# A decoder trunk in split float32: buffers of the MLP contraction laid where the next activations go, and pipelined quads

## The chip, the cores and the metric

The kernel runs on one core of a Trainium2 chip. The metric is the device time of one execution in microseconds (us); lower is better.

## What is computed

Two layers of a hybrid decoder act on a sequence of 1024 tokens with 1024 features, in float32. Both layers end in the same way; only that part is touched by the change.

```python
h = h + rmsnorm(m, ln_mix_post[layer])            # m: mixer output (attention, or a recurrence)
u = rmsnorm(h, ln_mlp_pre[layer])
f = jnp.square(jax.nn.relu(u @ mlp_w_up[layer])) @ mlp_w_down[layer]
h = h + rmsnorm(f, ln_mlp_post[layer])
e = rmsnorm(p[layer] @ ple_w_proj[layer], ple_norm[layer])
h = h + e * jax.nn.sigmoid(h @ ple_w_gate[layer])
```

`mlp_w_up` is 1024 x 4096, `mlp_w_down` 4096 x 1024, `ple_w_gate` 1024 x 1024.

## The kernel before, in words

**Split float32.** Every operand of a matmul is held as a high and a low part: ScalarE (ACT) casts it (line 117), VectorE (DVE) subtracts the cast from it (line 118). A product is then three matmuls, high-high, high-low and low-high (`mm3`, lines 149 to 151), each 128 x 128 by 128 x 512.

**Strassen-like MLP.** Both MLP products use a 2 x 2 block scheme with seven products in place of eight: A11, A12, S1, S2, S3, S4 and A22 name the sums of weight blocks, and the activations have seven matching factors (B11, B21, B22, T1 to T4). The factors of the input of the up product live in `comb`: four of them in the slots of the turned activations (`quart`, in the pool that `open_u` makes on the right side of the memory), three in the pool `ux`.

**Stages of one layer's end.** (1) `mix_out`: for each of eight token blocks `out_row` finishes the mixer's output product onto a partial sum loaded from memory, adds the residual and norms; `combine` turns the result by eight 128 x 128 transposes and writes factors into `comb`. Between them stand six products of the up stage, A11 and A12 of the first three of eight groups of 512 hidden features ("quads"): these three are *led*. A list, `plan`, sets the order in which these are written. (2) `mlp_up`: per quad seven products of 24 matmuls (five for a led quad). The two running banks are `b` and `c`; each value of `b` is read before the next product adds to it. DVE and ACT form hidden values, square them, form T1 to T4 and store all seven factors to memory (`keep`). For quads 0 and 1 `keep` splits each factor first into a pair of tiles `t` (three buffers) and stores both halves with DMAs that GpSimd (POOL) issues; for the others it stores the float32 tile with a DMA that SyncE (SP) issues. (3) `mlp_down`: four chunks of two quads, in the order 1, 2, 3, 0, seven products of 48 matmuls per chunk. `step` loads each factor, through a tile `c` and a split, or for chunk 0's quads as the stored pair; hidden tiles and half of the weights live in a pool `dn`, which is opened when `ux` and the activations' slots are closed. (4) gate: `add_norm` for all eight token blocks, their turning into fresh activation slots (`to_u`, 64 transposes, line 185), and 16 products of 24 matmuls, with a sigmoid behind each.

**What sets the order.** The kernel is written in one sequence, and a scheduler decides, per engine, the order in which instructions stand; each engine then runs its own in that order. A tile's buffer is given out again when its last reader is done. Four tiles `c0` to `c3` pass from hand to hand through a free list (`Free`); a led quad holds one for its partial sum `m1` and one for `u2`, and gives both back at its end. The scratch tiles of `mix_out` and the weight tiles of `mlp_up` (`wq`, `S`) share memory.

Of the kernel before, what the change touches and what calls it, by code (L numbers as in the profile page):

```python
# [17 lines left out]
P = 128  # L18
# [21 lines left out]
def tile_hybrid_trunk(  # L40
# [45 lines left out]
    def open_u(name, TA):  # L86
        up = tc.alloc_tile_pool(name=name, bufs=1, side="right", reuse_waits="tile")
        upools.append(up)
        for th, kh in ((1 - TA, 1), (1 - TA, 0), (TA, 1), (TA, 0)):
            quart[th, kh] = tuple(up.tile([P, 4, 512], F32R, name=f"u{x}{th}{kh}") for x in "hl")  # L90
# [88 lines left out]
    def to_u(tb, n):  # L179
        th, j = divmod(tb, 4)  # L180
        for hf in range(2):
            tp = any_bank()
# [719 lines left out]
    class Layer:  # L902
        def __init__(self, layer, TA, last):
# [5 lines left out]
            self.hidS = {(i, q): [dram.tile([P, D], F32R, name=f"hid{x}{layer}_{i}_{q}") for x in "hl"]  # L909
                         for i in range(7) for q in range(2)}  # L910
# [11 lines left out]
        def mix_out(self, wap, kpairs, src, part, order):  # L922
# [11 lines left out]
            with tc.tile_pool(name=f"pre{layer}", bufs=1, reuse_waits="tile") as mp:  # L934
                wslots.append((mp, "wBh", "wBl", 1, 1))
                wcount[0] = 0
                gains = [mp.tile([P, D], F32, name="gain", bufs=2) for _ in range(2)]
                bcast_row(gains[0], ln_mix_post[layer:layer + 1, :])
                w = [[stage_k(wap, r, 2, nh * 512, 512) for r in kpairs] for nh in range(2)]
# [6 lines left out]
                def out_row(tb):  # L946
                    a = mp.tile([P, D], F32, name="a", bufs=3)
                    nc.sync.dma_start(out=a, in_=part[tb])
# [9 lines left out]
                    vec(a, acc, a, ALU.add)  # L958
# [7 lines left out]
                def combine(tb):  # L966
# [23 lines left out]
                    vec(t1, p1, s1, ALU.subtract)  # L990
                    nc.scalar.copy(out=t3, in_=p1)
# [3 lines left out]
                    split(H[B22], L[B22], p2)  # L995
                    split(H[T3], L[T3], t3)
                    vec(t4, s2, t2, ALU.subtract)
                    split(H[T1], L[T1], t1)
                    split(H[T4], L[T4], t4)

                leads = []
                for q in range(NLEAD):
                    leads += self.lead_steps(q, mp)
                plan = [(out_row, 0), (out_row, 1), (combine, 0), (out_row, 2), (combine, 1), (out_row, 3),
                        (combine, 2), (out_row, 4), (combine, 3), (out_row, 5), None, (combine, 4),
                        (out_row, 6), None, (combine, 5), (out_row, 7), None, (combine, 6), None, None, None,
                        (combine, 7)]
                for step in plan:
                    if step is None:
                        leads.pop(0)()  # L1010
                    else:
                        step[0](order[step[1]])
                del wslots[3:]
# [26 lines left out]
        def loader(self, view, place):  # L1040
            got = {}

            def A(m, k):
                if (m, k) not in got:
                    pool, name, nb = place(m, k)
                    t = pool.tile([P, WE if name == "wraw" else D], F32, name=name, bufs=nb)[:, 0:D]
# [47 lines left out]

# [133 lines left out]
        def mlp_down(self, macc):  # L1228
# [5 lines left out]
            for c in range(chunks):  # L1234
                if c:
                    self.begin(c)
# [178 lines left out]
```

## Time and profile before

| quantity | value |
|---|---|
| median of 3 runs | 2764.43 us (2760.29 to 2765.16) |
| the profiled execution's own time | 2754.74 us |
| its span, first to last instruction | 2752.9 us |
| TensorE (PE) busy | 2531.9 us, 92% of the span |
| DVE, ACT, POOL busy | 60%, 46%, 10% |
| mean granted TensorE clock | 0.964 |

A wait row names who waited, for which engine's result, and then the total in us, how often, and the longest. In a timeline row the bracket at the end is the idle time of the engine just before that instruction, and what ended it. A window row gives the busy time of each engine in that stretch. The granted clock of 1.00 is 2.4 GHz, 0.50 is 1.2 GHz.

### The profile page before, as it was taken

How to read it: one execution, taken by the hardware profiler on the slowest of the kernel's cores; microseconds unless marked ns; L12 is line 12 of the kernel's file. 1: busy time of each engine (PE TensorE's matmuls, PEld its weight loads, DVE VectorE, ACT ScalarE, POOL GpSimd, SP SyncE). 2: the span in 40 equal slices, each digit the busy share in tenths (PEclk: the TensorE clock that was granted, in tenths of full speed). 3: DMA queues.
4: the chain of work that ended last, by engine and by line, in shares of the span. 5: the costliest groups of instructions: out<-in, count | busy, mean ns of one | idle time of the engine just before them, and what ended most of it. 6: DMA issues, size and time to landing. Idle time of an engine off the chain costs nothing. (4 is left out here: it accounts for less than half of the span.)

```text
span 2752.9 us, 31458 instructions
## 1 busy us (share of the span) xinstructions
PE 2531.9 (92%) x11681; PEld 2051.0 (75%) x11681; DVE 1656.4 (60%) x2075; ACT 1266.9 (46%) x1867; POOL 274.4 (10%) x422
## 2 busy tenths in 40 slices
PE   8899999987869998999989999997879998999989
PEld 7687888765657776777868788876657776777867
DVE  5565666665757555667564455645757555677562
ACT  4454556654535444333333366554535444433331
POOL 1312233211011000000200000001011000000210
PEclk9999999988889999999999999998889999999999
DMA  4756543335556437442753321245656437442752
GB/s 155 211 152 186 174 128 120 115 115 214 206 176 222 153 124 281 160 145 85 251 193 116 135 78 58 92 146 200 205 176 222 153 130 282 154 145 81 254 193 99
DMA packets 236733, 446.24 MB, mean 162 GB/s; under 512 B 17939, under 2 KB 125564, under 8 KB 236580
## 3 DMA queue, kind: packets, MB, share of 16 engines
q1 hardware_dynamic: 220452, 385.51, 42.2%
q0 software_dynamic: 16128, 58.73, 6.4%
q8 instruction: 92, 1.51, 0.2%
q14 instruction: 61, 0.50, 0.1%
HBM read 301.94 MB, written 142.23 MB: 161 GB/s over the span
## 5 line engine op out<-in xcount | busy, mean ns | idle before, releaser
L150 PE MATMUL sc<-wAl,hh 128*128 128x512 f32 x864 | 346.6, 401 | 7.5 <-DVE wAl L118 7.4
L149 PE MATMUL sc<-wAh,hh 128*128 128x512 f32 x864 | 333.4, 398 | 17.0 <-ACT wAh L117 15.9
L151 PE MATMUL sc<-wAh,hl 128*128 128x512 f32 x864 | 344.0, 398 | 0.0
L149 PE MATMUL sc<-xh,wAh 128*128 128x512 f32 x384 | 158.3, 412 | 65.9 <-DVE c L878 35.9
L149 PEld LDWEIGHTS sc<-wAh,hh 128*128 128x128 f32 x864 | 163.3, 189 | 59.9 <-ACT wAh L117 17.5
L150 PEld LDWEIGHTS sc<-wAl,hh 128*128 128x128 f32 x864 | 163.4, 189 | 58.9 <-DVE wAl L118 20.8
L149 PE MATMUL sc<-uh,wAh 128*128 128x512 f32 x464 | 185.6, 400 | 9.0 <-ACT wAh L117 9.0
L151 PEld LDWEIGHTS sc<-wAh,hl 128*128 128x128 f32 x864 | 163.5, 189 | 37.1
L150 PE MATMUL sc<-ul,wAh 128*128 128x512 f32 x464 | 183.8, 396 | 0.0
L151 PE MATMUL sc<-uh,wAl 128*128 128x512 f32 x464 | 183.1, 395 | 0.0
L117 ACT CAST hh<-c 128x1024 fp32r<-128x1024 f32 x80 | 83.6, 1048 | 203.7 <-PE sc L150 190.4
L118 DVE TENSOR_TENSOR wAl<-wraw,wAh 128x1024 fp32r<-128x1024 f32 (+1 forms) x94 | 120.4, 1282 | 94.4 <-ACT wAh L117 94.0
L151 PE MATMUL sc<-xh,wAl 128*128 128x512 f32 x384 | 154.4, 404 | 2.8 <-DVE wAl L118 2.8
L118 DVE TENSOR_TENSOR wAl<-wq,wAh 128x1024 fp32r<-128x1024 f32 x80 | 97.6, 1220 | 96.7 <-ACT wAh L117 96.6
L117 ACT CAST wAh<-wraw 128x1024 fp32r<-128x1024 f32 (+1 forms) x94 | 98.5, 1048 | 124.2 <-PE sc L150 45.6
L150 PE MATMUL sc<-xl,wAh 128*128 128x512 f32 x384 | 155.2, 404 | 0.0
L118 DVE TENSOR_TENSOR hl<-c,hh 128x1024 fp32r<-128x1024 f32 x80 | 97.5, 1220 | 95.3 <-ACT hh L117 95.3
L117 ACT CAST wAh<-wq 128x1024 fp32r<-128x1024 f32 x80 | 83.8, 1047 | 137.9 <-PE sc L150 132.1
L149 PEld LDWEIGHTS sc<-xh,wAh 128*128 128x128 f32 x384 | 74.5, 194 | 92.1 <-issue 36.7
L149 PE MATMUL mm<-uh,wAh 128*128 128x512 f32 x312 | 126.8, 406 | 9.7 <-ACT st L344 7.4
L404 DVE CUSTOM_DVE_ANT_0 sn<-sc,bias 128x128 f32<-128x128 f32 (+7 forms) x128 | 94.4, 753 | 55.2 <-PE tp L421 23.6
L150 PE MATMUL mm<-ul,wAh 128*128 128x512 f32 x312 | 124.5, 399 | 0.0
(415 smaller groups left out, 6311.8 us busy)
## 6 DMA issues: line engine op xcount, KB each, us to landing
c<-hid SPq DMA_DIRECT2D x84, 512.0 KB
wq<-in_mlp_w_up_dram SPq DMA_DIRECT2D x44, 512.0 KB
hid<-row SPq DMA_DIRECT2D x38, 512.0 KB
wraw<-in_mlp_w_up_dram SPq DMA_DIRECT2D x32, 512.0 KB
hD<-row SPq DMA_DIRECT2D x32, 512.0 KB
hidh<-t POOLq DMA_DIRECT2D x28, 512.0 KB, 3.2
hidl<-t POOLq DMA_DIRECT2D x28, 512.0 KB, 3.5
hh<-hidh POOLq DMA_DIRECT2D x28, 512.0 KB, 5.0
```

Source lines behind the costliest of these rows:

```text
L117: nc.scalar.copy(out=dst_h, in_=src)
L118: nc.vector.tensor_tensor(out=dst_l, in0=src, in1=f32(dst_h), op=ALU.subtract)
L149: nc.tensor.matmul(dst, lh, rh, start=start, stop=False, skip_group_check=onto)
L150: nc.tensor.matmul(dst, lh, rl, start=False, stop=False, skip_group_check=onto)
L151: nc.tensor.matmul(dst, ll, rh, start=False, stop=stop, skip_group_check=onto)
L404: nc.vector.tensor_tensor_reduce(out=sn[:, :w], in0=sps[:, :w], in1=bias, scale=-1.0, scalar=BIG, op0=ALU.add, op1=ALU.min, accum_out=nm)
```

## The change

It does six things in each layer's end. (a) `out_row` loads the partial sum into a tile `c2` or `c3`, not into the tile `a` that later holds the result; a third `out_row` stands ahead of the first `combine`, and `combine` splits in another order. (b) `early_s1` prepares the S1 weights of quad 0 in `mix_out`, from tiles that are free there, and quad 0 runs S1 before S2. (c) Quads are pipelined: A11 of the next quad stands between S3 and A22 of this one. (d) No factor is stored as a pair: all go out as float32 through SP, and the last chunk of the contraction splits its factors like the others; chunks go 0, 1, 2, 3, and T4 gets a tile of its own. (e) The contraction's hidden tiles and one weight pair use the slots of the next activations, its banks have a pool of their own (`k0` to `k3`), and its first product is issued before the old pools are closed. (f) In the last chunk half of the token blocks are normed after A22 and turned between the last products; the gate norms and turns only the other half, two products after the start.

```diff
-                    a = mp.tile([P, D], F32, name="a", bufs=3)
-                    nc.sync.dma_start(out=a, in_=part[tb])
+                    pt = self.cpool.tile([P, D], F32, name=f"c{2 + tb % 2}", bufs=1)
+                    nc.sync.dma_start(out=pt, in_=part[tb])
...
-                plan = [(out_row, 0), (out_row, 1), (combine, 0), (out_row, 2), (combine, 1), (out_row, 3),
+                plan = [(out_row, 0), (out_row, 1), (out_row, 2), (combine, 0), (out_row, 3), (combine, 1),
...
+                        self.early_s1, (combine, 7)]
...
+        def early_s1(self):
+            A = self.loader(self.up_view(0), lambda m, k: (wpool, "wraw", 2))
+            s1 = A(1, 0)
+            vec(s1, s1, A(1, 1), ALU.add)
+            self.w_s1 = self.weights({"S1": lambda: s1}, "S1", A, None)
...
                     def keep(i, t):
-                        if q >= 2:
-                            nc.sync.dma_start(out=self.hidD[i][q], in_=t)
-                            return
-                        h, l = (hp.tile([P, D], F32R, name="t", bufs=3) for _ in range(2))
-                        split(h, l, t)
-                        for d, s in zip(self.hidS[i, q], (h, l)):
-                            nc.gpsimd.dma_start(out=d, in_=s)
+                        nc.sync.dma_start(out=self.hidD[i][q], in_=t)
...
+                    c = pair_bank()
+                    if q == 0:
+                        product(c, "S1", True)
                     product(b, "S2", led)
+                    running(u2)
+                    if q:
+                        product(c, "S1", True)
+                    product(b, "S3", False)
+                    running(u3)
+                    if q + 1 < quads:
+                        start(q + 1)
...
-                    product(c, "S4", False)
+                    product(c, "S4", False, self.first_step if q == quads - 1 else None)
...
-                    vec(c21, c21, t2, ALU.subtract)
-                    keep(T4, c21)
+                    t4 = hp.tile([P, D], F32, name="t", bufs=3)
+                    vec(t4, c21, t2, ALU.subtract)
+                    keep(T4, t4)
...
-            self.chunk = ((2 * c + 2) % (FF // 512), (2 * c + 3) % (FF // 512))
+            self.chunk = (2 * c, 2 * c + 1)
...
+                    slot = (f"uh{TB}1", f"ul{TB}1", f"uh{TB}0", f"ul{TB}0")[self.turn % 4]
+                    both = upools[-1].tile([P, 2, D], F32R, name=slot, bufs=1)
...
                 for jj, b in product("A22", 0, False):
                     onto((0, 1), jj, b, True)
+                    if final:
+                        norms([4 * TA + 2 * jj + r for r in range(2)], rows)
...
+                if final:
+                    turns(1)
+                for jj, b in product("S4", 1, False):
...
+                    if final:
+                        turns(2 - jj)
...
+            bank0 = {}
+            for jj in range(2):
+                b = bank0[0, jj] = self.down_bank(jj).rearrange("p (r d) -> p r d", d=512)
+                self.down_product(self.ops0, b, jj, True)
             self.xpool.release()
             close_u()
...
+                if nh == 0:
+                    norms(order[4:], rows)
...
+                    if nh == 0:
+                        need_u([order[n + 3]] if 1 <= n < 5 else [])
```

TensorE at the end of layer 0's `mix_out`, before (`tp<-ident,a` is the last `combine`; factors `xh`, `xl` are T2, `uh_131`, `ul_132` are T1):

```order
L151 MATMUL sc<-uh_133,wAl 128x512
L975 MATMUL tp<-ident,a 128x128 x8
L149 MATMUL sc<-xh_7569,wAh 128x512
L150 MATMUL sc<-xl_7570,wAh 128x512
L149 MATMUL sc<-uh_131,wAh 128x512
L150 MATMUL sc<-ul_132,wAh 128x512
L151 MATMUL sc<-xh_7569,wAl 128x512
```

and with the change:

```order
L156 MATMUL sc<-uh_133,wAl 128x512
L979 MATMUL tp<-ident,a 128x128 x8
L154 MATMUL sc<-uh_131,wAh 128x512
L155 MATMUL sc<-ul_132,wAh 128x512
L156 MATMUL sc<-uh_131,wAl 128x512
```

The first product after the last turning was S2, which reads T2 and whose weights are a sum of three loads; now a whole S1, which reads T1, stands there first.

DVE at the end of quad 0 and up to the read of quad 1's first bank, before (`c_8428` is quad 0's hidden block B12 in the making, `c_7998` its B21, `t` the pairs that are stored; `c_8646<-sc,c_8217` is quad 1's `u2`):

```order
L118 TENSOR_TENSOR t<-row,t 128x1024
L118 TENSOR_TENSOR wAl<-wraw,wAh 128x1024
L878 TENSOR_TENSOR t<-c_8428,row 128x1024
L878 TENSOR_TENSOR c_8428<-row,c_8428 128x1024
L878 TENSOR_TENSOR row<-row,t 128x1024
L118 TENSOR_TENSOR t<-t 128x1024
L878 TENSOR_TENSOR c_7998<-c_7998,row 128x1024
L118 TENSOR_TENSOR wAl<-wq,wAh 128x1024
L118 TENSOR_TENSOR t<-c_8428,t 128x1024
L118 TENSOR_TENSOR t<-row,t 128x1024
L118 TENSOR_TENSOR t<-c_7998,t 128x1024
L878 TENSOR_TENSOR c_8646<-sc,c_8217 128x1024
```

and with the change (`c_8442`, `c_7976` and `c_8598<-sc,c_8197` are the same three; the first row reads S4's bank):

```order
L883 TENSOR_TENSOR c_8442<-sc,c_8442 128x1024
L123 TENSOR_TENSOR wAl<-wq,wAh 128x1024
L123 TENSOR_TENSOR wAl<-wraw,wAh 128x1024
L883 TENSOR_TENSOR t<-c_8442,row 128x1024
L883 TENSOR_TENSOR wq<-wq,S 128x1024
L883 TENSOR_TENSOR c_8442<-row,c_8442 128x1024
L883 TENSOR_TENSOR t<-row,t 128x1024
L123 TENSOR_TENSOR wAl<-wq,wAh 128x1024
L883 TENSOR_TENSOR t<-c_7976,t 128x1024
L883 TENSOR_TENSOR c_8598<-sc,c_8197 128x1024
```

Every `t<-...,t` of the old piece is the low half of a split; the new piece has none, and its `t` are T1, T2 and T4 themselves.

## Rows read from the trace of the kernel before

**Rows 1.** Busy time by window: start:end, length, PE, PEld, DVE, ACT, POOL, clock, DMA.
```profile
636.00:736.60 100.60, 90.48 (x401) 73.13 (x401) 69.53 (x77) 53.84 (x98) 12.45 (x17) 0.92 0.59 216
736.60:748.10 11.50, 0.01 (x1) 0.00 (x0) 9.00 (x12) 5.34 (x10) 0.00 (x0) 0.70 0.68 228
748.10:813.20 65.10, 42.54 (x168) 32.65 (x169) 42.19 (x37) 22.20 (x22) 7.68 (x14) 0.81 0.59 194
851.50:1067.00 215.50, 210.07 (x889) 166.28 (x890) 113.17 (x96) 100.20 (x98) 2.65 (x5) 1.00 0.47 167
1067.00:1084.50 17.50, 10.68 (x46) 8.29 (x45) 9.53 (x8) 8.04 (x8) 0.00 (x0) 0.94 0.68 248
1286.00:1399.00 113.00, 111.26 (x473) 88.64 (x474) 72.83 (x64) 38.29 (x49) 20.14 (x34) 1.00 0.64 214
1399.00:1418.20 19.20, 10.63 (x58) 9.35 (x56) 17.35 (x21) 10.79 (x21) 1.42 (x3) 0.70 0.68 229
...
2636.70:2655.30 18.60, 10.71 (x58) 8.63 (x56) 17.37 (x21) 11.31 (x21) 1.45 (x3) 0.74 0.72 253
```

**Rows 2.** Waits of PE over the whole span: total us, times, longest.
```profile
PE sc L149 <- DVE c L878: 35.9, 2, 20.2
PE tp L975 <- DVE a L176: 23.5, 3, 8.5
PE tp L185 <- DVE ul L118: 15.8, 7, 4.6
```

**Rows 3.** Timeline of PE, layer 0: start us, duration us, engine, line, instruction.
```profile
735.57 1.03 PE L975 MATMUL tp<-ident,a 128*128 128x128 f32 x8
748.14 0.80 PE L149 MATMUL sc<-xh,wAh 128*128 128x512 f32 x1 [11.54 <-ACT wAh L117]
...
763.41 0.40 PE L149 MATMUL sc<-xh,wAh 128*128 128x512 f32 x1
...
813.21 0.77 PE L149 MATMUL sc<-xh,wAh 128*128 128x512 f32 x1 [20.15 <-DVE c L878]
...
874.01 0.40 PE L149 MATMUL sc<-xh,wAh 128*128 128x512 f32 x1
...
879.61 0.40 PE L151 MATMUL sc<-uh,wAl 128*128 128x512 f32 x1
...
891.41 0.49 PE L149 MATMUL sc<-uh,wAh 128*128 128x512 f32 x1 [0.90 <-ACT wAh L117]
...
1084.55 1.22 PE L149 MATMUL sc<-wAh,hh 128*128 128x512 f32 x2 [6.87 <-ACT wAh L117]
```

**Rows 4.** Timeline of DVE, layer 0, quads 0 and 1.
```profile
760.07 1.22 DVE L878 TENSOR_TENSOR wq<-wq,S 128x1024 f32<-128x1024 f32 x1 [3.73 <-DMA wq<-in_mlp_w_up_dram]
761.22 1.22 DVE L878 TENSOR_TENSOR c<-sc,c 128x1024 f32<-128x1024 f32 x1
...
785.91 1.22 DVE L878 TENSOR_TENSOR c<-sc,c 128x1024 f32<-128x1024 f32 x1
...
810.58 1.23 DVE L118 TENSOR_TENSOR t<-c,t 128x1024 fp32r<-128x1024 f32 x1 [4.79 <-DMA hidh<-t]
811.84 1.22 DVE L878 TENSOR_TENSOR c<-sc,c 128x1024 f32<-128x1024 f32 x1
```

**Rows 5.** Waits of ACT from 780 to 815 us.
```profile
ACT t L117 <- DMA hidl<-t: 12.7, 3, 5.9
```

**Rows 6.** DMA issues: size each, median us from issue to landing.
```profile
hidh<-t POOLq DMA_DIRECT2D x28, 512.0 KB, 3.2
```

**Rows 7.** Timeline of DVE in layer 0's mix_out.
```profile
681.15 1.23 DVE L878 TENSOR_TENSOR a<-sc,a 128x1024 f32<-128x1024 f32 x1 [3.23 <-DMA a<-part]
```

**Rows 8.** The page's costliest groups: count, busy us, mean ns, idle before.
```profile
L117 ACT CAST hh<-c 128x1024 fp32r<-128x1024 f32 x80 | 83.6, 1048 | 203.7 <-PE sc L150 190.4
L118 DVE TENSOR_TENSOR hl<-c,hh 128x1024 fp32r<-128x1024 f32 x80 | 97.5, 1220 | 95.3 <-ACT hh L117 95.3
```

**Rows 9.** Waits of the DMA queue SP from 736 to 850 us.
```profile
SPq L1048 <- DVE wAl L118: 83.3, 9, 34.5
```

More of the change, by code (lines that the diff above doesn't have):

```diff
@@ L1104, in new @@
                     return self.mw.tile([P, D], F32, name="S", bufs=4)
[L1106 to L1129 removed]
+                started = {}
@@ new lines, in start @@
+                def start(q):
+                    A, sums = self.loader(self.up_view(q), place), {}
+                    if q in self.lead:
+                        started[q] = (A, sums, None) + self.lead.pop(q)
+                        return
+                    b = pair_bank()
+                    self.up_product(b, self.weights(sums, "A11", A, new), "A11", True, True)
+                    m1n, m1 = self.c.take()
+                    nc.scalar.copy(out=m1, in_=b)
+                    started[q] = (A, sums, b, m1n, m1)
@@ new lines, in quad, with product, running @@
+                def quad(q):
+                    A, sums, b, m1n, m1 = started.pop(q)
+                    led = b is None
+                    def product(bank_, name, start, before=None):
+                        w = self.w_s1 if q == 0 and name == "S1" else self.weights(sums, name, A, new)
+                        if before:
+                            before()
+                        self.up_product(bank_, w, name, start, True)
+                    def keep(i, t):
+                        nc.sync.dma_start(out=self.hidD[i][q], in_=t)
+                    def running(dst):
+                        if led:
+                            vec(dst, b, m1, ALU.add)
+                        else:
+                            nc.scalar.copy(out=dst, in_=b)
+                    if not led:
@@ L1307, in mlp_and_ple @@
             pairs[0] = 2
-            open_u(f"ug{layer}", 1 if last else 0)
-            order = [4 * TA + j for j in range(4)] + [4 * (1 - TA) + j for j in range(4)]
-            with tc.tile_pool(name=f"gt{layer}", bufs=1, reuse_waits="tile") as mp:
-                wslots.extend([(self.mw, "wq", "S", 4, 4)] * 4)
-                wcount[0] = 3
-                (_, g1), (_, g2), (_, j1), (_, j2) = [self.c.take() for _ in range(4)]
-                bcast_row(g1, ln_mlp_post[layer:layer + 1, :])
-                if not last:
-                    bcast_row(g2, ln_mix_pre[layer + 1:layer + 2, :])
-                halves = [j[:, i * 512:(i + 1) * 512] for j in (j1, j2) for i in range(2)]
+            fill_u(TB)
@@ new lines, in mlp_and_ple @@
+            order = [4 * TA + j for j in range(4)] + [4 * TB + j for j in range(4)]
+            wslots.extend([(self.mw, "wq", "S", 4, 4)] * 4)
+            wcount[0] = 3
+            (_, j1), (_, j2) = self.c.take(), self.c.take()
+            if not last:
+                g2 = self.c.take()[1]
+                bcast_row(g2, ln_mix_pre[layer + 1:layer + 2, :])
+            halves = [j[:, i * 512:(i + 1) * 512] for j in (j1, j2) for i in range(2)]
+            for nh in range(2):
+                cs = slice(nh * 512, (nh + 1) * 512)
+                w = [stage_k(ple_w_gate[layer], kb, 2, nh * 512, 512) for kb in range(0, KB, 2)]
+                if nh == 0:
+                    norms(order[4:], rows)
+                    for tb, h in normed:
+                        to_u_later(tb, h)
```

258 lines of the change are left out of this document (131 added, 127 removed).

## Prediction, before the run

> **What bounds the kernel now.** I read the shares of busy time first: TensorE is busy for 92% of the span and no other engine for more than 60%, so the time is TensorE's matmuls plus whatever TensorE loses. The change hardly alters the matmuls (the same products, the same 64 turnings per gate), so only the losses can move. Next I read busy time by window, cut at the seams of layer 0's stages [rows 1], and TensorE's waits [rows 2], to see at which seam the loss lies. At the full clock 24 matmuls take 5.60 us: one product begins at 874.01, the next at 879.61 [rows 3]. Against that measure:
>
> - `mix_out` (636.0 to 736.6) has one wait of some 8 us in layer 0; both layers together 23.5 us in three waits, the longest 8.5, for the normed row `a` [rows 2].
> - From the last turning (8 transposes, 735.57 on) to quad 0's first matmul at 748.14 TensorE idles 11.54 us [rows 3]; the same seam in layer 1 is alike.
> - Quad 1 waits once 20.15 us for `c` [rows 3]; over both layers 35.9 us in two waits, so layer 1's is 15.7 [rows 2].
> - From 851.5 to 1067.0 stand 37 products (five quads of seven and two more): 37 x 5.60 = 207.2 of 215.5 us, a loss of 8.3 [rows 1]. Once a quad TensorE idles 0.90 us [rows 3], where A22 must not add to `b` before it is read.
> - The contraction's second product waits 6.87 us [rows 3].
> - From the contraction's last matmul to the gate's first, 19.2 us pass (18.6 in layer 1) [rows 1] for 64 transposes, which at 1.03 us for eight [rows 3] need 8.2: 11.0 and 10.4 us are lost, which [rows 2] books in part to `ul`, the low half of the new slots.
>
> **Part by part.** Sums are over both layers, where a layer 1 figure is not shown it is taken equal to layer 0's.
>
> *(a) Partial sums in `c2`, `c3`.* DVE waited 3.23 us for such a load [rows 7], since it could start only once a `combine` had freed `a`. That goes. But with the change three turnings stand in one row behind the sixth `out_row`, and the third needs row 3, whose `a` comes free only with the first turning. From there it takes, in DVE's order, the addition, two turnings' splits, two scalings of other rows and its own three passes, at 1.2 us a pass about as long as before. I keep one wait of 8.5 per layer: 23.5 - 17.0, **6.5 us gained**, all in layer 1. Ends: 0 and 17.
>
> *(b) S1 first.* S1 reads T1, which is split first: two DVE passes and a cast after the last turning (735.57 + 1.03), so it can start some 2.7 us behind it, near 739.3, in a gap that held nothing. The gain is less than S1's 5.6 us, though. S2's weights come no earlier, and behind S2 stands S3, which may not start before `u2` has read the bank; S1 used to stand between them as cover. In DVE's order that read follows a weight sum that waited 3.73 us for its load (760.07), so it ran at 761.22 to 762.4 [rows 4] and S3 began at 763.41 [rows 3]. With S1 over by 747, the weights of A22 find their buffer earlier, the load behind them too, and I put S3 near 760.7: 2.7 per layer, **5.4 gained**. Ends: 0 and 11.2.
>
> *(c, d) The slot wait.* Quad 1's `u2` needs the tile that held quad 0's `m1`, which is free when T4 has been split and the pair formed (810.58 to 811.81); the read of the bank follows at 811.84 and TensorE at 813.21 [rows 3, 4]. Quad 0's last bank was read at 785.91 [rows 4]: 26 us for a tail of seven splits through three `t` buffers, each waiting for the store of an earlier half; ACT alone waited 12.7 us in three waits for `hidl` [rows 5], DVE up to 4.79 for `hidh` [rows 4]. With the change the tail is, in DVE's order, ten rows (the read of S4's bank to `u2`), at 1.2 us 11.7, plus some 1.2 of ACT's squaring that nothing covers: 13 us. TensorE has half of S2 and all of S1 of quad 1 meanwhile, 2.8 + 5.6 = 8.4 us. A wait of 4.6 remains per layer: 35.9 - 9.2 = **26.7 gained**. Ends: 18 (each remaining wait 9) and 36.
> The stores of this stretch leave POOL for SP. A POOL store took 3.2 us to land [rows 6]. The Trainium skill ("DMA: Bandwidth & Descriptors", section "Issuing engines are not separate DMA queues") says that DMAs of all issuing engines run on the same 16 DMA engines, so that the choice of engine saves only the time of issuing. By that rule a store lands no sooner from SP; if the landing were the limit, the sum would be 44 in place of 70.7. I keep 26.7, since a quad now takes three `t` tiles, one store each, in place of fourteen halves: no buffer has a second use within a quad.
>
> *(c) Pipelined quads.* A11 of the next quad, 5.6 us, covers the read of `b` before A22 (about 1 us of ACT or DVE). Of 8.3 lost I leave 2: **12.6 gained**. Ends: 8 and 16.
>
> *(e) First product before the pools close, hidden tiles in slots that are free early.* A12's factors can be loaded and split while A11 runs (11.2 us of cover). Of the 6.87 I leave 1.4 for the new banks, whose predecessors must first be read: **11.0 gained**. S2's second pair of weights now stands on SP behind row loads that wait for quad 7's tail; it has two products, 22 us, of cover. Ends: 6 and 14.
>
> *(d) Splits in the last chunk.* 14 factors per layer arrive unsplit: 14 x 1.048 us on ACT and 14 x 1.220 us on DVE [rows 8], 14.7 and 17.1. From 1286 to 1399 ACT is busy 38 and DVE 73 of 113 us [rows 1], so there is room, but (f) puts four norms (two DVE passes, 2.45 us each) and four turnings' splits (eight passes of half the width) there as well, some 15 us of DVE. DVE comes to 105 of 113, and an in-order engine that full is late now and then: **8 lost**. Against this, the up stage loses 14 such splits per layer (counted above, in the tail). Ends: 0 and 16.
>
> *(f) Half of the rows turned early.* The gate can start on the four turned blocks; the other four are normed during its first 22 us. It starts when a bank is free, though. The first gate bank lies where `k0` lay, which is read last, after DVE's read of the contraction's last bank, a norm pass, two weight splits and two turned halves: about 6.3 us behind the last matmul. With the transposes that moved (they cost TensorE the same) I leave 5.5 and 5.4 lost of 11.0 and 10.4: **10.5 gained**. Ends: 0 and 18.
>
> *The clock.* The granted clock is 0.70 in both long gaps and 0.81 from 748.1 to 813.2 [rows 1]; the first matmuls behind a gap take 0.77 to 0.80 us, against 0.40 [rows 3], the lower of the two levels. Two of the gaps per layer shrink much; at an estimated 1.5 us each, **6 gained**. Ends: 0 and 12.
>
> Sum: 6.5 + 5.4 + 26.7 + 12.6 + 11.0 - 8.0 + 10.5 + 6.0 = 70.7. The profiled execution took 2754.74, so it would take 2684. The median shown, 2764.43, lies 9.7 above it; I predict the median, 2764.4 - 70.7 = **2693.7**, given as 2693.
>
> **The rivals.**
> *More comes back (2656).* The part loads clear the waits of (a) altogether (17 more), S1 pays its full 5.6 (6 more), the last chunk costs nothing (8), the clock gives 6 more: 2693 - 37. For it: DVE has 35% idle in the last chunk [rows 1], and each in-order delay above is my reading of an order, not a measured wait. Against: the chain behind row 3 is long in both orders.
> *Half of it stays (2725).* The remaining slot wait is 9 rather than 4.6 (9 less), the gate's bank wait eats all of (f) (10), the last chunk costs twice (8), S1 nothing (5): 2693 + 32. For it: all are in-order queues with DVE near its limit.
> *The landing is the limit (2720).* By the sharing of the DMA engines, worked out above, the slot wait stays: 2693 + 27. Against: ACT's waits were for a buffer's second use within one quad [rows 5], and that second use is gone.
> *Slower (2805).* One mechanism: SP issues in order, and per led quad seven, per layer 14 more, stores with a condition stand among the weight loads. SP already stood 83.3 us in 114 before up-weight loads, waiting for a buffer [rows 9]. If in each of the 16 quads one load stood behind a late store, it would cost a product the load's 3.7 us [rows 4] and the sum, cast and split behind it (3.5), 7 us: 16 x 7 = 112, against 70.7 gained, 2764 + 41. It decides once a load is more than a product (5.6 us) late. Against: the five later quads of a layer store through SP already and lose only 1.7 us each.
> *It does not do what it says.* If the scheduler undid the order: 2764. The instruction order shows the moved rows, so this gets 2%.
>
> **How the numbers follow.** Chances: forecast 0.50 (its own range 2675 to 2712), more 0.23, half 0.12, landing 0.07, slower 0.05, no change 0.03. From 2646 to 2730 lies all of the forecast and its three neighbours but their tails, with 0.8 in all. A measurement here can tell 0.2%, 5.5 us, from no change. Faster by more: 0.92; within: 0.03; slower: 0.05.
>
> **What would show it.** Right: no `t` split and no wait for `hidh` or `hidl` anywhere; TensorE's wait for `c` under 12 us in total; the five later quads at 39.5 us each; no wait above 3 us at the contraction's second product; 7 to 10 us from the contraction's last matmul to the gate's first; one wait of 7 to 9 us left in each `mix_out`. Wrong: SP-bound weight loads as releasers of TensorE's waits, waits of several us within the last chunk, or a slot wait of 15 us and more.

## The result, and the profile after

The changed kernel takes 2693.53 us (median of 4 runs, 2692.57 to 2697.95) where the kernel before takes 2762.36 (2759.89 to 2765.16, 4 runs): a ratio of 0.9754, 95% interval 0.9737 to 0.9771. It is faster, and the forecast was 2693. The profiled execution took 2697.95, with a span of 2695.8 us and a mean granted clock of 0.972, where it was 0.964. One run of a kernel below, the one without the pipelining, took 5090.92 us, nearly twice its others, for a cause that stays open; its median is taken without it. The page of the changed kernel, engines' busy time (us, share of the span, instructions):

```profile
PE 2519.5 (93%) x11681; PEld 2053.3 (76%) x11681; DVE 1653.8 (61%) x2077; ACT 1265.1 (47%) x1867; POOL 218.5 (8%) x310
```

TensorE does the same work in a span that is 57 us shorter. To see where, both traces are cut into windows at the same matmuls, counted from the last turning of each `mix_out`: the 312th, 1200th, 1344th and 2496th matmul behind it, and the gate's first. Layer 0, the last stretch of layer 1 and the two gates in the kernel before (start:end, length, PE, PEld, DVE, ACT, POOL, clock, DMA):

```profile
736.60:850.47 113.87, 78.01 (x313) 60.55 (x313) 75.61 (x70) 45.30 (x49) 12.48 (x23) 0.85 0.59 193
850.47:1066.36 215.89, 210.16 (x888) 166.04 (x889) 114.19 (x97) 101.10 (x99) 2.65 (x5) 1.00 0.48 168
1066.36:1110.98 44.62, 36.21 (x144) 28.05 (x143) 32.71 (x29) 17.30 (x18) 0.00 (x0) 0.92 0.79 294
1110.98:1385.09 274.11, 271.54 (x1152) 214.78 (x1150) 181.99 (x157) 105.17 (x115) 18.45 (x32) 1.00 0.50 163
1385.09:1418.18 33.09, 22.99 (x108) 18.71 (x107) 27.48 (x30) 15.99 (x30) 3.11 (x4) 0.83 0.67 232
...
1418.18:1975.36 557.18, 535.39 (x2336) 431.65 (x2336) 300.17 (x323) 283.64 (x400) 23.47 (x40) 0.97 0.37 126
2622.84:2655.30 32.46, 23.03 (x109) 18.00 (x107) 27.50 (x30) 16.54 (x30) 3.11 (x4) 0.85 0.70 244
2655.30:2747.89 92.59, 92.59 (x392) 74.30 (x392) 24.84 (x36) 12.31 (x20) 0.00 (x0) 0.98 0.31 106
```

The same windows in the changed kernel:

```profile
747.94:845.71 97.77, 82.08 (x314) 63.43 (x313) 61.59 (x57) 31.78 (x34) 0.00 (x0) 0.91 0.46 159
845.71:1054.98 209.27, 207.45 (x889) 166.66 (x888) 111.27 (x94) 99.83 (x99) 0.00 (x0) 1.00 0.46 165
1054.98:1098.92 43.94, 36.24 (x145) 27.87 (x143) 30.05 (x26) 16.89 (x17) 0.00 (x0) 0.92 0.62 227
1098.92:1368.22 269.30, 269.30 (x1157) 216.46 (x1155) 198.05 (x172) 118.58 (x130) 5.20 (x4) 1.00 0.47 149
1368.22:1391.86 23.64, 15.48 (x80) 12.48 (x78) 20.66 (x22) 11.64 (x21) 2.15 (x3) 0.91 0.72 245
...
1391.86:1952.64 560.78, 539.00 (x2362) 433.61 (x2360) 309.90 (x334) 289.11 (x410) 26.30 (x42) 0.98 0.39 131
2573.21:2596.07 22.86, 15.25 (x79) 12.29 (x77) 20.42 (x22) 11.39 (x21) 2.21 (x3) 0.92 0.74 244
2596.07:2690.91 94.84, 94.84 (x418) 76.29 (x416) 32.66 (x45) 16.89 (x29) 2.47 (x2) 0.98 0.40 130
```

With layer 1 cut in the same way (its five stretches take 113.02, 215.86, 44.55, 274.05, 32.46 before and 96.15, 210.75, 44.14, 269.53, 22.86 after), the account of both layers is, in us:

| stretch | before | after | gained | the prediction's terms |
|---|---|---|---|---|
| last turning and first 13 products of the up stage | 226.9 | 193.9 | 33.0 | (b) 5.4, slot wait 26.7 |
| its last 37 products | 431.8 | 420.0 | 11.7 | (c) 12.6 |
| contraction's first 3 products | 89.2 | 88.1 | 1.1 | (e) 11.0 |
| its next 24 products | 548.2 | 538.8 | 9.3 | (d) -8.0 |
| its last product, to the gate's first matmul | 65.6 | 46.5 | 19.1 | (f) 10.5 |
| gate to the next last turning, gate to the end | 649.8 | 655.6 | -5.8 | (a) 6.5 |

The clock's 6.0 lie spread over these rows and are not measured by themselves: the granted clock rises from 0.85 to 0.91 in the first and from 0.83 to 0.91 in the fifth. The sum is 68.4 against a predicted 70.7. The last row also holds layer 1's mixer, which the change does not touch. Before layer 0's last turning the changed kernel stands 11.3 us later (747.94 against 736.60); the first experiment shows what that is. TensorE's waits in the changed kernel, over the whole span:

```profile
PE sc L154 <- DVE c L883: 14.7, 4, 5.1
PE k L155 <- DVE wAl L123: 14.0, 4, 6.1
PE k L190 <- DVE ul L123: 14.0, 2, 7.3
PE tp L979 <- DVE a L181: 10.7, 2, 5.4
...
PE sc L154 <- ACT wBh L122: 7.9, 2, 6.4
```

The wait for `c`, 35.9 us before [rows 2], is 14.7; for `a` it was 23.5 and is 10.7; for `ul` at a turning it was 15.8 in seven waits and is 14.0 in two. Two rows are new: weights `wAl` at the contraction (bank `k`), and `wBh`, the output product's weights. TensorE's timeline in layer 0, with the waits for `c` of layer 1 at its end, puts them in their places:

```profile
746.91 1.03 PE L979 MATMUL tp<-ident,a 128*128 128x128 f32 x8
750.63 0.51 PE L154 MATMUL sc<-uh,wAh 128*128 128x512 f32 x1 [2.69 <-ACT uh L122]
...
771.93 0.47 PE L154 MATMUL sc<-xh,wAh 128*128 128x512 f32 x1 [2.08 <-DVE c L883]
...
808.25 0.76 PE L154 MATMUL sc<-xh,wAh 128*128 128x512 f32 x1 [5.08 <-DVE c L883]
...
1391.09 1.12 PE L190 MATMUL k<-ident,row 128*128 128x128 f32 x4 [7.26 <-DVE ul L123]
1391.86 0.78 PE L154 MATMUL tp<-wq,uh 128*128 128x512 f32 x1
...
1978.52 0.77 PE L154 MATMUL sc<-xh,wAh 128*128 128x512 f32 x1 [4.03 <-DVE c L883]
...
2012.70 0.77 PE L154 MATMUL sc<-xh,wAh 128*128 128x512 f32 x1 [3.47 <-DVE c L883]
```

S1 starts 2.7 us behind the last turning, S3 24.0 (26.8 before, by [rows 3]), and quad 1's wait for a free tile is 5.08 where it was 20.15. In layer 1 S3 starts 25.9 us behind the last turning (1952.64 to 1978.52), only 1.0 us earlier than before, and quad 1's wait is 3.47 where it was 15.7. So the four waits for `c` are two of S3 in quad 0 (2.08 and 4.03) and two of quad 1. VectorE's tail in layer 0, from the read of S4's bank to quad 1's `u2`:

```profile
794.80 1.22 DVE L883 TENSOR_TENSOR c<-sc,c 128x1024 f32<-128x1024 f32 x1 [5.58 <-PE sc L156]
...
806.88 1.22 DVE L883 TENSOR_TENSOR c<-sc,c 128x1024 f32<-128x1024 f32 x1
```

That is 13.3 us to the end of the last row, where the prediction put 13 and the kernel before took 26. From quad 1's wait to the contraction TensorE has no gap of more than 1.9 us.

### The profile page after: what moved, and what is told of

Same layout as the page of the kernel before. It is cut to its first block, busy times and chain, and to the rows that moved or that the text cites. A ratio compares the mean times of both kernels' runs of the same rounds, so it can differ in the third digit from the quotient of the medians.

```text
span 2695.8 us, 31246 instructions
## 1 busy us (share of the span) xinstructions
PE 2519.5 (93%) x11681; PEld 2053.3 (76%) x11681; DVE 1653.8 (61%) x2077; ACT 1265.1 (47%) x1867; POOL 218.5 (8%) x310
## 5 line engine op out<-in xcount | busy, mean ns | idle before, releaser
L122 ACT CAST wAh<-wq 128x1024 fp32r<-128x1024 f32 x110 | 115.3, 1048 | 302.6 <-PE k L156 153.2
L123 DVE TENSOR_TENSOR wAl<-wq,wAh 128x1024 fp32r<-128x1024 f32 x110 | 134.3, 1221 | 150.5 <-ACT wAh L122 150.5
L892 POOL TENSOR_TENSOR rs<-ms,nhalf 128x1 f32<-128x1 f32 x56 | 50.7, 911 | 1832.1 <-ACT ms L890 1832.0
L155 PE MATMUL k<-wAl,uh 128*128 128x512 f32 x464 | 185.3, 399 | 12.2 <-DVE wAl L123 12.2
L154 PE MATMUL k<-wAh,uh 128*128 128x512 f32 x464 | 182.7, 399 | 2.8 <-ACT wAh L122 1.4
L156 PE MATMUL k<-wAh,ul 128*128 128x512 f32 x464 | 183.6, 396 | 0.0
L154 PE MATMUL sc<-xh,wAh 128*128 128x512 f32 x384 | 158.1, 412 | 25.6 <-DVE c L883 14.7
L155 PE MATMUL k<-wAl,ul 128*128 128x512 f32 x432 | 171.5, 397 | 1.8 <-DVE wAl L123 1.8
L156 PE MATMUL k<-wAh,uh 128*128 128x512 f32 x432 | 172.6, 400 | 0.5 <-DVE uh L123 0.5
L154 PE MATMUL k<-wAh,ul 128*128 128x512 f32 x432 | 166.9, 396 | 0.0
L122 ACT CAST wAh<-S 128x1024 fp32r<-128x1024 f32 x62 | 65.1, 1050 | 189.3 <-PE sc L155 93.3
L154 PE MATMUL mm<-uh,wAh 128*128 128x512 f32 x312 | 127.9, 410 | 10.5 <-ACT st L349 8.2
L156 PE MATMUL mm<-uh,wAl 128*128 128x512 f32 x312 | 124.7, 400 | 0.0
```

What stands on the lines that cost most here:

```text
L122: nc.scalar.copy(out=dst_h, in_=src)
L123: nc.vector.tensor_tensor(out=dst_l, in0=src, in1=f32(dst_h), op=ALU.subtract)
L154: nc.tensor.matmul(dst, lh, rh, start=start, stop=False, skip_group_check=onto)
L155: nc.tensor.matmul(dst, lh, rl, start=False, stop=False, skip_group_check=onto)
L156: nc.tensor.matmul(dst, ll, rh, start=False, stop=stop, skip_group_check=onto)
L892: nc.gpsimd.tensor_tensor(out=rs, in0=ms, in1=nhalf, op=ALU.pow)
```

## The experiments

Every kernel was timed beside the kernel before, in four series in which that one's median lay from 2755.69 to 2758.79. The changed kernel was timed again in the first of them, with a ratio of 0.9763 (0.9741 to 0.9785); what is said below in us against it compares medians across series.

**Once more, unchanged.** No edit.

> The changed kernel itself once more, for a second profile. In its first profile the first output row began at 649.3 us, in that of before at 638.2, though TensorE's order up to there is the same but for a few rows. Theory: the 11 us are no part of the change but scatter of the attention stage; the row then begins anywhere from 635 to 650 here, and the median stays within 4 us of 2693.5. Rival: the weights of the output product now go into another slot first, and the start waits for it; then the row begins at 648 to 651 again, and the change hides a loss of 8 to 11 us.

Median 2693.72. The profile's start is 9.5 us shorter than that of the first one, while the two stretches of MLP and the gates agree within 1.7 us (642.3 and 642.9 from last turning to gate, where the first profile has 643.9 and 643.4):

```profile
0.00:738.44 738.44, 663.50 (x3753) 569.20 (x3753) 467.95 (x958) 401.02 (x835) 175.67 (x254) 0.96 0.53 162
738.44:1380.74 642.30, 610.13 (x2577) 486.77 (x2577) 421.66 (x370) 278.81 (x298) 7.30 (x7) 0.98 0.48 164
```

So the 11 us are scatter of the attention stage; in the profiles of all kernels here the last turning of layer 0's `mix_out` ends between 736.6 and 747.9 us, and the changed kernel's first profile is the latest. The rival holds in small: the first output row does wait for `wBh`, 1.50 us in both profiles, and 6.4 to 6.5 in layer 1.

**The parts undone one by one.** Pipelining:

```diff
-                    if q + 1 < quads:
-                        start(q + 1)
...
-                start(0)
                 for q in range(quads):
+                    start(q)
                     quad(q)
```

> The changed kernel, with the next quad's A11 back behind this quad's last product. Theory: each of the ten later quads then waits again for the read of b before A22; the prediction gave the pipelining 12.6 us of 16.6 lost, and the changed kernel's later quads show no wait at all, so 13 to 17 us come back: 2706 to 2711, with a wait of 0.9 us and the lower rate behind it in every later quad. Rival: these losses went with the split copies and the stores' move; then within 4 us of the changed kernel, 2690 to 2698.

Median 2701.88 of five, ratio 0.9802 (0.9779 to 0.9826): 8 us slower by the medians, short of the 13 to 17 expected, and 12 to 14 by the two MLP stretches of its profile (649.7 each, against those of either profile above). TensorE's waits in it from 830 to 1060 us show what came back:

```profile
PE sc L154 <- ACT wAh L122: 4.5, 5, 0.9
PE sc L154 <- ACT row L1152: 2.5, 5, 1.8
```

Five waits of 0.9 us in five quads, as before; the rival falls.

S1 behind S2 in quad 0:

```diff
-                        self.early_s1, (combine, 7)]
+                        (combine, 7)]
...
-                        w = self.w_s1 if q == 0 and name == "S1" else self.weights(sums, name, A, new)
+                        w = self.weights(sums, name, A, new)
...
-                    c = pair_bank()
-                    if q == 0:
-                        product(c, "S1", True)
...
-                    if q:
-                        product(c, "S1", True)
+                    c = pair_bank()
+                    product(c, "S1", True)
```

> The changed kernel without the early S1 weights: quad 0 runs S2 before S1 like the others. Theory: S1 in front is worth only what S3 starts earlier, 2.7 us per layer, so 2699 (2696 to 2702); the gap behind the last turning is 11 us again. Rival one: it is worth its whole product, 5.6 per layer, 2705. Rival two: S3 waits for the same chain on VectorE in both orders and it is worth nothing, 2693.

Median 2698.23, ratio 0.9791 (0.9768 to 0.9814): 4.5 us slower by the medians, with intervals that overlap; by the profiles 7 to 9, since both MLP stretches (647.3 and 647.2 us) are 3 to 5 us longer, where those of the changed kernel's two profiles differ by 1.6 at most. The gap behind the last turning is 11.34 us again. By the profiles, that it is worth nothing is out; between 2.7 and 5.6 us per layer the runs don't decide.

Norms and turnings all behind the contraction (`norms` and `turns` taken out of the last chunk):

```diff
+            for tb in order:
+                norms([tb], rows)
+                to_u_later(*normed.pop())
+                drain(1)
             for nh in range(2):
```

> The changed kernel with all eight norms and turnings behind the contraction again. Theory: the gap from the contraction's last matmul to the gate's first grows from 9 to about 19 us per layer, of which the transposes that move with it need 4; the last chunk gains nothing, since it showed only one wait of 0.9 us: 10 to 14 us slower, 2704 to 2708. Rival one: the norms in the last chunk did cost there, as the prediction's 8 us for that chunk say, and it comes out even, 2693 to 2698. Rival two: the gap was closed by the banks' new pool and the slots laid out early, not by the early turning; then also even, with a gap of 9 to 11 us.

Median 2706.51, ratio 0.9823 (0.9802 to 0.9845): 13 us slower. From the contraction's last matmul to the gate's first it takes 16.2 us (17.9 in layer 1), the changed kernel 9.1 (8.5). Both rivals fall. In its last chunk, which now has less to do, TensorE waits where the changed kernel does not (timeline of PE):

```profile
1369.70 0.80 PE L155 MATMUL k<-wAl,ul 128*128 128x512 f32 x1 [4.04 <-DVE wAl L123]
```

**Part (d) alone, on the kernel before.** The factors of quads 0 and 1 go out in float32; in the second kernel POOL issues those stores (`nc.gpsimd` where q < 2). With the pairs go the second storing of B11 in these quads and T2's use of B11's tile, and the contraction loads and splits all factors alike.

```diff
-                        if q >= 2:
-                            nc.sync.dma_start(out=self.hidD[i][q], in_=t)
-                            return
-                        h, l = (hp.tile([P, D], F32R, name="t", bufs=3) for _ in range(2))
-                        split(h, l, t)
-                        for d, s in zip(self.hidS[i, q], (h, l)):
-                            nc.gpsimd.dma_start(out=d, in_=s)
+                        nc.sync.dma_start(out=self.hidD[i][q], in_=t)
```

> The kernel before with part (d) of the change alone: the factors of quads 0 and 1 go out as one float32 tile through SP and are split when the contraction loads them. Theory: quad 1's wait for a free c tile came from the tail of splits through three t buffers; with the tail down to 13 us that wait falls from 35.9 to about 9 us over both layers, less some us for the splits in the last chunk: 19 to 27 us faster than before, a ratio of 0.990 to 0.993. Rival (the transfers' landing is the limit, whichever engine issues): the wait for c stays above 25 us and the time within 6 us of before.

> The same, but the stores of quads 0 and 1 are still issued by POOL. Theory (the second use of a buffer within one quad was the limit, not the issuing engine): within 5 us of the float32 version through SP, wait for c again about 9 us. Rival (POOL's issue path was the limit): the wait for c is 20 us or more and the time lies 10 to 27 us above the version through SP. Second rival (SP's queue suffers from the stores): this one is faster than the version through SP by 5 us or more.

Ratios to before 0.9984 (0.9972 to 0.9996) and 0.9985 (0.9973 to 0.9998). The wait for `c`, through SP and then through POOL:

```profile
PE sc L149 <- DVE c L878: 14.6, 2, 7.4
```

```profile
PE sc L149 <- DVE c L878: 16.8, 2, 8.9
```

The pairs were the cause of the wait: 21 us of 35.9 went with them, and 19 where POOL issues the stores. Which part of a pair it was, the split passes, the second store or a buffer's second use, is not separated, since they went together. The issuing engine was not the limit, nor was a single store's landing: POOL's stores took 3.3 to 3.8 us to land in the second kernel, no less than the 3.2 of [rows 6]. The Trainium skill ("DMA: Bandwidth & Descriptors", section "Issuing engines are not separate DMA queues") says that the choice of engine saves no more than the time of issuing. The two times agree with that, 0.9984 against 0.9985. But of the 19 to 27 us expected only 4 arrive. From last turning to gate the kernel that stores through SP gains 3.8 us in each layer (677.80 and 676.17 us), and its last chunk shows where the rest went (waits of PE, 1290 to 1402 us):

```profile
PE sc L150 <- DVE wAl L118: 4.7, 4, 3.9
PE sc L149 <- ACT wAh L117: 1.0, 1, 1.0
```

Behind the 13th product it is 11.2 us ahead in layer 0 and 10.8 in layer 1; that shrinks in the last chunk, where the kernel before has waits of 1.8 us in place of these 5.7, and at the gate's start. The releasers say that TensorE waits there for splits of weights; that these are late because the factors' splits stand among them on VectorE is argued.

**The new waits.** First `wBh`, with the slot last in the ring again:

```diff
-                wslots.insert(0, (mp, "wBh", "wBl", 1, 1))
+                wslots.append((mp, "wBh", "wBl", 1, 1))
```

> The changed kernel with the slot wB last in the ring of weight slots again, not first. Theory: the waits for wBh before the first output row (7.9 us in both layers, 6.4 of it in layer 1) come from that order alone and go: 5 to 8 us faster than the changed kernel, ratio to before 0.973 to 0.975. Rival one: the wait only passes to another weight or to the led products that then use wB's place later: within 3 us. Rival two: the old order blocks the next stage's weights: slower by 3 us or more.

Median 2691.44, ratio 0.9762 (0.9742 to 0.9782): the same as the changed kernel. Rival one holds for the time. The 6.4 us are gone: from the mixer's last matmul to the last turning layer 1 takes 100.7 us, in the changed kernel 106.4. But the stretch from there to the gate takes 646.4, where the changed kernel's two profiles have 643.4 and 642.9. S2's weights are part of that (waits of PE, 1850 to 1960 us):

```profile
PE sc L154 <- ACT wAh L122: 4.0, 1, 4.0
PE sc L156 <- DVE wAl L123: 2.4, 1, 2.4
```

Both stand behind the last turning, where the changed kernel waits for the same weights, 2.7 and 2.7 us in its first profile and 0.7 and 2.9 in its second. What else lengthens that stretch is open.

Next the contraction's 6.1 us. VectorE ahead of S2 in the changed kernel:

```profile
1073.88 1.23 DVE L123 TENSOR_TENSOR ul<-c,ul 128x1024 fp32r<-128x1024 f32 x1 [3.19 <-ACT ul L122]
1075.02 1.22 DVE L883 TENSOR_TENSOR S<-wraw,uh 128x1024 f32<-128x1024 f32 x1
...
1079.56 1.22 DVE L883 TENSOR_TENSOR wq<-wq,wraw 128x1024 f32<-128x1024 f32 x1
1080.69 1.22 DVE L883 TENSOR_TENSOR wq<-wq,S 128x1024 f32<-128x1024 f32 x1
...
1085.23 1.22 DVE L123 TENSOR_TENSOR wAl<-S,wAh 128x1024 fp32r<-128x1024 f32 x1
```

It idles 3.19 us at a hidden split, and the sums for S3 and S4 (1079.56, 1080.69) stand ahead of the second pair's split at 1085.23. One kernel gives the A22 weights of chunk 0 another slot:

```diff
-                            self.w22 = upools[-1].tile([P, 2, D], F32, name=f"uh{self.TA}0", bufs=1)
+                            self.w22 = upools[-1].tile([P, 2, D], F32, name=f"uh{1 - self.TA}0" if c == 0 else f"uh{self.TA}0", bufs=1)
```

> The changed kernel, but in the contraction's first chunk the weight pair A22 takes the slot in which factor T1 of the up stage lay (free since quad 7's S1), and a hidden tile takes the slot that the first contraction product frees. Theory: S2's wait (6.1 us per layer, the new loss of the contraction) hangs on that slot, which comes free only when the first product ends at 1066.2; with the weights loaded before, the wait falls under 2 us per layer: 8 to 12 us faster than the changed kernel, ratio 0.972 to 0.974. Rival: VectorE's eleven passes without a gap between 1074 and 1086 set it, not the slot; then the wait stays above 4 us per layer and the time within 4 us.

Median 2689.30, ratio 0.9753 (0.9732 to 0.9773), and the wait is 6.13 us as before: what gain the median may hold does not come from there. Nor does the run test the slot. SP issues the load of that weight pair in the changed kernel and here at

```profile
1066.84 1.36 SPq L1056 DMA_DIRECT2D uh<-in_mlp_w_down_dram  x2
```

```profile
1059.09 1.40 SPq L1056 DMA_DIRECT2D uh<-in_mlp_w_down_dram  x2
```

and the second product starts at 1067.02 and at 1059.26: the load goes 0.2 us ahead of it in both, each time directly behind a factor's load on SP, so it was no earlier for the new slot.

A second also loads them early, through POOL, forms the sums S1 and S2 of both quads before the second product's factors are split (`behind` is the last of them, later S2's last split), and keeps the rest behind; what is written in an `issue_after` block stays behind the instruction named, in that engine's order:

```diff
+            for A in self.As:
+                A(1, 1)
             ul0 = up.tile([P, 4, 512], F32R, name=f"ul{TA}0")
...
+                    eng = nc.gpsimd if queue and (m, k) == (1, 1) else nc.sync
...
+                    if c == 0 and name == "A12":
+                        for s in self.sums:
+                            for k in ("S1", "S2"):
+                                if callable(s[k]):
+                                    s[k] = s[k]()
+                        behind = latest["vec"]
+                    if c == 0 and name in ("S2", "S3", "S4"):
+                        with tc.issue_after(behind):
+                            ops = self.step(name)
```

> The changed kernel, in the contraction's first chunk: the A22 weights lie in the slot that is free early and are loaded through POOL, the sums S1 and S2 of both quads stand on VectorE ahead of S2's hidden splits, and the sums S3 and S4 behind S2's last split. Theory: the 6.1 us of wait at S2, which laying the slot free alone did not touch, come from VectorE's order (3.4 us idle for a hidden split with the sums behind it, four passes for later products in front); put in order, the wait falls under 1.5 us: 9 to 12 us faster than the changed kernel over both layers, ratio 0.972 to 0.973. Rival: twelve passes are too many for the 11.2 us of one product in any order, and the wait stays above 4 us.

Median 2683.78, ratio 0.9740 (0.9716 to 0.9764). In layer 0 the wait is 0.6 us, in layer 1 still 4.0: the theory holds in the one layer and for a third in the other, where POOL's load went no earlier than before (2257.06, with the second product at 2257.67).

The gate's start. In the changed kernel's ScalarE timeline a cast of later weights (1388.13) stands ahead of the turned blocks (1389.28):

```profile
1388.13 1.04 ACT L122 CAST wAh<-wraw 128x1024 fp32r<-128x1024 f32 x1 [3.65 <-DMA wraw<-in_ple_w_gate_dram]
...
1389.28 1.05 ACT L122 CAST uh<-k 128x512 fp32r<-128x512 f32 x2
```

```diff
+                    with tc.issue_after(self.turned[0]), tc.issue_after(self.turned[1]):
+                        w = [stage_k(ple_w_gate[layer], kb, 2, nh * 512, 512) for kb in range(0, KB, 2)]
```

> The changed kernel, with the gate's second half of weights queued behind the last early turning on ScalarE and VectorE. Theory: the 9 us from the contraction's last matmul to the gate's first are not the bank as such but ScalarE's order: a cast of gate weights that are needed 45 us later stands ahead of the casts that read the turned blocks, and itself waits 3.7 us for its load. With it behind, the wait of 7 us at the last turning falls to 2 to 4 us: 6 to 10 us faster than the changed kernel over both layers, ratio to before 0.973 to 0.974. Rival: VectorE, with norms and sums in front, is as late as ScalarE; the wait stays above 5 us, the time within 3 us.

Median 2690.74, ratio 0.9761 (0.9742 to 0.9780): nearer the rival. The wait falls only from 14.0 to 10.4 us over both layers (4.4 and 6.0), and the time stays within 3 us.

Both edits together, without further change:

> Both of these together. Theory: they lie at two seams 310 us apart and add up: 15 to 20 us faster than the changed kernel, 2674 to 2679 where that takes 2693.5, ratio to before 0.969 to 0.971. Rival: what the contraction gains at its start it loses again at its end, in VectorE's queue; then no more than the better of the two alone.

Median 2680.23, ratio 0.9722 (0.9704 to 0.9740): 13 us below the changed kernel's median. The two edits add up, 9.9 and 3.0 us by the medians where each stands alone; the 15 to 20 expected are missed because each gave less than forecast. Its two layers differ; POOL's and VectorE's timelines say how:

```profile
1029.73 1.65 POOL L1062 DMA_DIRECT2D uh<-in_mlp_w_down_dram  x2 [299.71 <-PE sc L158]
```

```profile
2257.20 1.52 POOL L1062 DMA_DIRECT2D uh<-in_mlp_w_down_dram  x2 [328.85 <-PE k L158]
```

```profile
2265.86 1.23 DVE L888 TENSOR_TENSOR S<-wraw,uh 128x1024 f32<-128x1024 f32 x1 [5.52 <-DMA uh<-in_mlp_w_down_dram]
```

In layer 0 an up product (`sc`) set the slot free, in layer 1 the contraction's own first product (`k`), and VectorE idled 5.52 us for the load. So in layer 1 alone the slot was named after that of the low half `ul0`:

```diff
-            for A in self.As:
-                A(1, 1)
+            if layer == 0:
+                for A in self.As:
+                    A(1, 1)
             ul0 = up.tile([P, 4, 512], F32R, name=f"ul{TA}0")
+            if layer == 1:
+                for A in self.As:
+                    A(1, 1)
```

> The combined kernel, with one line moved in layer 1: the slot for the A22 weights is laid out behind another, so that it comes to lie on the low half of factor T1 there too. In layer 1 of the combined kernel POOL's load of these weights went only when the first contraction product had read that memory (2257.2), VectorE then idled 5.5 us and TensorE waited 4.0 us at S2; in layer 0 the load went at 1029.7 and the wait was 0.6. Theory: slots of the new pool lie in memory in the order in which they are first named, whatever their names, so with another order layer 1 behaves as layer 0: load near 2225, wait under 1 us, 2 to 4 us faster than the combined kernel, ratio to before 0.970 to 0.972. Rival: the load is held by something else in layer 1; nothing changes.

Median 2677.45 (2674.07 to 2681.17), ratio 0.9709 (0.9695 to 0.9722). POOL's load in layer 1, and TensorE's longest wait there from 2245 to 2290 us:

```profile
2224.13 1.52 POOL L1062 DMA_DIRECT2D uh<-in_mlp_w_down_dram  x2 [299.22 <-PE sc L158]
```

```profile
PE k L157 <- DVE wAl L123: 0.9, 2, 0.6
```

This version beats both kernels: some 15 us below the changed one by median and by ratio, with 634.5 and 634.4 us from last turning to gate (643.9 and 643.4 in the changed kernel's first profile).

## Why the prediction was right, point by point

**Held.** *Slot wait*: 4.6 us were left per layer by the forecast; 5.08 in layer 0 and 3.47 in layer 1 are, 27.3 gained of 26.7. The reason held too: the tail on VectorE is 13.3 us, forecast 13, and without the pairs the wait shrinks under either issuing engine. *(c)*: 11.7 gained of 12.6, and undoing it costs 8 to 14. Its reason is told too simply, though. The 0.90 us of [rows 3] are booked to a weight cast; the copy of `b` stands behind that cast on ACT, and A22 starts when it ends:

```profile
891.26 1.01 ACT L1149 COPY row<-sc 128x1024 f32<-128x1024 f32 x1
```

```profile
892.32 0.50 PE L149 MATMUL sc<-xh,wAh 128*128 128x512 f32 x1 [0.18 <-ACT row L1149]
```

*(b)*, in layer 0 alone: S3 came 2.8 us earlier behind the last turning, forecast 2.7; in layer 1 it came 1.0 earlier (0.3 in the second profile). *Rivals*: the landing as the limit falls with the two float32 kernels; behind quad 1 no wait of TensorE in the up stage is above 1.9 us, so the slower rival's mechanism does not appear either.

**Signs.** No pair is stored and no wait for one is left; the later quads take 39.6 us each in layer 0 (37 products in 209.27) and 39.9 in layer 1, forecast 39.5; the contraction's second product waits 0.7; the gap to the gate is 9.1 and 8.5. Two signs failed: the wait for `c` is 14.7 in place of under 12, because S3 in quad 0 now waits for it too, and in each `mix_out` there are waits of 5.4 and 2.8 in place of one of 7 to 9. The chance of no change is given as 2% in one place and as 0.03 in another; the sum of the chances uses 0.03.

**Wrong, and cancelling.** Four terms missed, two in each direction.

- *(e), forecast 11.0, found 1.1.* The step that failed is the sentence that S2's second pair of weights "has two products, 22 us, of cover". The 6.87 us of the second product [rows 3] became 0.7, but S2 waits 6.1. With the sums in order and the slot early, that wait is 0.6 (layer 0 of the second kernel above); with the order alone 4.0 (its layer 1). The 6.1 are thus in part VectorE's order and in part a slot that only the first product frees. What an early load without the new order would give was not run.
- *(d), forecast -8.0, found +9.3 in its stretch.* The loss is real where (d) stands alone, 3.9 us in one wait; in the full change the last chunk has one wait of 0.9 us, though VectorE is busier over the stretch (198 of 269 us against 182 of 274). Over the 24 products TensorE idled 2.6 us in layer 0 before and not at all after; the rest of the gain there is a shorter busy time. Part (e) gave this stretch other banks and slots as well, so the row is not (d)'s alone. Why norms put in early cost nothing there, where the same norms at the end go with a weight split that is 4.0 us late (norms undone), no run isolates.
- *(f), forecast 10.5 with part of the clock's 6.0, found 19.1.* The gap to the gate's first matmul was forecast at 7 to 10 and is 9. But the idle time in this stretch fell only from 10.1 to 8.2 us in layer 0 and from 9.4 to 7.6 in layer 1; the rest is busy time, 23.0 to 15.5 with 28 rows fewer in layer 0. What was left out: the transposes that moved go off this seam, where the granted clock was 0.83, and their cost appears in the gate instead, at 0.98, with 26 more rows there and 2.2 us more in layer 1's, where TensorE waits 0.6 us before and not at all after. Nor is it the gate's first bank that sets the start, as the prediction had it: the last early turning waits (7.26 and 6.7 us), and the gate follows it at once.
- *(a), forecast 6.5, found -5.8 with the gates.* In layer 1 the stretch from the first output row to the last turning fell from 104.5 to 99.8 us, but its start now waits 6.4 us for `wBh`, which the prediction did not price: it took the slot's new place in the ring for free. Put back, this stage is 5.7 us shorter and the next one some 3 longer. The one wait of 8.5 us per layer is 5.4, with another of 2.8 for the copy of a turned half. Of the rest of the -5.8, 2.2 are the last gate, (f)'s transposes, and the stretch with the mixer differs by 1.6 us between the changed kernel's own two profiles.

So the total was right to a microsecond by compensation, which is luck, while the two largest terms, the slot wait and the pipelining, were right by themselves.

## What to carry to other kernels

A loss at a seam belongs to the seam: price what the next step there needs (here S2's sums) before booking the gain, since covering one product's operands may only move the wait to the next product. A part that removes work from one place and puts it at another (the pairs) can be worth 21 us on the wait that it targets and 4 us in the total; run it alone before crediting it. Where a wait on an in-order engine is suspected, look at what stands in front that is not needed yet, and at the slot that the operand's load needs: here the order alone took a third of the wait, both together nearly all of it.

## What the runs showed that was not expected

- A slot's name says nothing about its memory: slots of a new pool seem to be laid over the old one in the order in which they are first named. The one moved line bears this out: it took a load in layer 1 from 0.6 us ahead of the second product (2257.20 to 2257.81) to 30.7 us ahead of it (2224.13 to 2254.81). No address was read. That the new name alone changed nothing has another reason besides: there the load stood in SP's queue.
- Two profiled executions of the same program differ by 9.5 us before layer 0's last turning and by 1.7 us or less in each later stretch. A difference of this size in the attention stage need not be an effect of an edit.
- Issued through POOL while SP issued loads of hidden factors, a pair of 512 KB weight loads reached VectorE 8.7 us after issue (2257.20 to 2265.86). The 3.7 us that the prediction took for one such load [rows 4] are VectorE's wait for it and not its time from issue.
